# Interleaved stationary operands and a moving operand read from last to first, in a float32r decoder block on one core

## The chip, the cores and the metric

The kernel runs on one core of a Trainium2 chip. The metric is device time in microseconds (us) of one execution; times shown are the median of several runs. The profile shows one execution with every instruction on each engine: PE is the matmul engine (TensorE), PEld its loads of the stationary operand, ACT is ScalarE, DVE is VectorE, POOL is GpSimd, SPq the queue from which most DMAs are issued.

## The reference

One decoder layer over 256 tokens with a model width of 2048, all in float32. In order:

```python
x = x + 0.5 * swiglu(rmsnorm(x, ffn1_norm[i]), ffn1_w_gate[i], ffn1_w_up[i], ffn1_w_down[i])
h = rmsnorm(x, mix_norm[i])
proj = h @ w_in[i]
dq, dk, dv, hq, hf, hi, hg, gate_a, gate_b = jnp.split(proj, split_points, axis=-1)
...
y_a = diff_attention(dq, dk, dv, q_norm[i], k_norm[i], lam, rel_bias, diff_subln[i], lambda_init)
y_b = hgrn2(hq, hf, hi, hg, lower_bounds[i], hgrn_norm[i])
merged = jax.nn.sigmoid(gate_a) * (y_a @ w_branch_a[i]) + jax.nn.sigmoid(gate_b) * (y_b @ w_branch_b[i])
x = x + merged @ w_out[i]
x = x + 0.5 * swiglu(rmsnorm(x, ffn2_norm[i]), ffn2_w_gate[i], ffn2_w_up[i], ffn2_w_down[i])
ple = rmsnorm(p[i] @ w_ple_proj[i], ple_post_norm[i])
x = x + jax.nn.sigmoid(rmsnorm(x, ple_gate_norm[i]) @ w_ple_gate[i]) * ple
```

The feed-forward width is 5632; attention and the gated recurrence (hgrn2) have 8 heads of width 128 each.

## The kernel before

**Tiling.** Every large product has 256 tokens, in two token tiles of 128 (`NT`, index `tt`), and streams its weights from memory in blocks of 256 x 512 numbers (512 KB): two k tiles (`k2`) of 128 rows, 512 output columns (`NB`). The activations are the stationary operand, 128 features x 128 tokens for a k tile and a token tile; the weights are the moving operand, 128 x 512, read from column 0 to 511; the result, 128 tokens x 512 columns, gathers in one PSUM bank (`acc`).

**Precision.** Each number is split into a high float32r part and the rest. ScalarE writes the high part (`wh` for weights, line 114; names in H such as `AH`, `hH`, `yaH`, `ybH`, `mH`, `pH` for activations), VectorE the rest (`wl`, line 115; names in L). A product takes three matmuls: high by high (line 148), high by low (149), low by high (150).

**Order.** The schedule is written by hand. A table, `plan`, lists all 804 blocks in the order of their use: gate and up of the first feed-forward part (`gu1`, 176 blocks), `down1` (88), the columns of `w_in` for the mixing part (18 chunks of 8 blocks), `w_a` (16), then `w_in` and `w_b` by turns (32 and 16), `w_out` (32), `gu2` (176), `down2` (88), and `w_pg` and `w_pp` for the embedding (32 and 4). `prep` brings a block in and splits it `AHEAD` = 3 blocks before `group` multiplies it with 12 matmuls. Between blocks, small tasks (evacuations, transposes, attention heads, recurrence levels) are advanced by one step each.

**The last product.** Column chunk 3 of `w_pg` is done by `last_product`: there the second token tile goes in two halves of 256 columns into banks of the pool `ms`, so its matmuls read 128 x 256 moving columns.

**Layout of the stationary operands.** `new_act` and others allocate a tile [128, k tiles, 256 tokens]: the 128 tokens of a token tile lie side by side, 4 bytes apart, 512 bytes for a token tile. They are written by `split` (lines 182 to 187) from a PSUM bank of transposed activations (`tp`), or at the start from the tile `junk` that holds the transposed input. `two_k_tiles` calls `split` for two k tiles at once (512 elements for a partition) where there is no gain, for one (256 elements) where there is. `branch_input` (lines 358 to 364) calls it with a gain for two k tiles at once.

Of the kernel before, what the change touches and what calls it, by code (L numbers as in the profile page):

```python
# [11 lines left out]
F32R = mybir.dt.float32r  # L12
# [8 lines left out]
P = 128  # L21
SEQ = 256
NT = SEQ // P
D = 2048
KD = D // P
DFF = 5632
NH = 8
# [21 lines left out]
def block_kernel(ctx: ExitStack, tc: tile.TileContext, a: dict, out: bass.AP):  # L49
    nc = tc.nc  # L50
# [11 lines left out]
    def T(pool, shape, tag, dt=F32, **kw):  # L62
        uid[0] += 1
        return pool.tile(shape, dt, tag=tag, name=f"{tag}_{uid[0]}", **kw)

    def tcol(tt):
        return slice(tt * P, (tt + 1) * P)

    def ccol(c):
        return slice(c * NB, (c + 1) * NB)  # L70


    plan = []

# [63 lines left out]

    WHOLE = slice(0, NB)

    def group(n, act, last, dsts):
        AH, AL = act
        wh, wl = ready[n]
        for k2 in range(2):
            kt = 2 * plan[n][2] + k2
            for dst, tt, cols in dsts:
                hi, lo = AH[:, kt, tcol(tt)], AL[:, kt, tcol(tt)]
                nc.tensor.matmul(dst, hi, wh[:, k2, cols], start=(kt == 0), stop=False)  # L148
                nc.tensor.matmul(dst, hi, wl[:, k2, cols], start=False, stop=False)  # L149
                nc.tensor.matmul(dst, lo, wh[:, k2, cols], start=False, stop=(kt == last))  # L150

    def stream(w, c, groups, act, dsts, held=0):
        for g in range(groups - held):
# [25 lines left out]


    def split(H, L, src, gain=None):
        if gain is None:
            nc.scalar.copy(H, src)  # L183
            nc.vector.tensor_tensor(L, src, H.bitcast(F32), op=ALU.subtract)  # L184
        else:
            nc.scalar.activation(H, src, AF.Copy, scale=gain)  # L186
            nc.vector.scalar_tensor_tensor(L, src, gain, H.bitcast(F32), op0=ALU.mult, op1=ALU.subtract)
# [32 lines left out]
        return tp  # L220

    def new_act():
        return T(base, [P, KD, SEQ], "AH", F32R), T(base, [P, KD, SEQ], "AL", F32R)

    def new_ss4():
        return T(base, [P, NT, 4], "ss4", bufs=2)
# [19 lines left out]

    def ffn(gu, down, act, gain_next):
        with tc.tile_pool(name=gu, bufs=1) as fp:
            hH = T(fp, [P, DFF // P, SEQ], "hH", F32R)
            hL = T(fp, [P, DFF // P, SEQ], "hL", F32R)  # L250

            def hidden(acc, c):
                if c == 0 and rs[0] is None:
                    early = T(fp, [P, NT, NB], "early")
                    for tt in range(NT):
                        nc.scalar.copy(early[:, tt, :], acc[tt])
                    acc = [early[:, tt, :] for tt in range(NT)]
                while rs[0] is None:
                    yield
                h = []  # L260
                for tt in range(NT):
                    s = T(fp, [P, HALF], "s", bufs=2)
                    nc.scalar.activation(s, acc[tt][:, :HALF], AF.Silu, scale=rs[0][:, tt : tt + 1])  # L263
                    h.append(T(fp, [P, HALF], "h", bufs=4))
                    nc.vector.scalar_tensor_tensor(  # L265
                        h[tt], acc[tt][:, HALF:], rs[0][:, tt : tt + 1], s, op0=ALU.mult, op1=ALU.mult
                    )
                yield
                two_k_tiles(lambda tt, kt: h[tt][:, (kt - 2 * c) * P : (kt - 2 * c + 1) * P], hH, hL, 2 * c)

            for c in range(DFF // HALF):
                acc = product(gu, c, KG, act)
                spawn(hidden(acc, c))
            nact = new_act()
            ss4 = new_ss4()
            for c in range(D // NB):
                acc = product(down, c, FG, (hH, hL))
                spawn(residual(acc, c, 0.5, ss4, nact, gain_next, set_rs if c == 3 else None))
        return nact
# [51 lines left out]
    mp = mid.enter_context(tc.tile_pool(name="mid", bufs=1))  # L331
    GA = T(mp, [P, NT, D], "GA")
    V = T(mp, [P, NT, NH * VD], "V")
    yaH = T(mp, [P, NH, SEQ], "yaH", F32R)
    yaL = T(mp, [P, NH, SEQ], "yaL", F32R)
    nc.vector.tensor_scalar(gsub, small[:, S_SUB : S_SUB + 1], 1.0 - LAMBDA_INIT, None, op0=ALU.mult)

    def mix(m):
# [2 lines left out]
    def rcol(tt):  # L341
        return rs[0][:, tt : tt + 1]
# [14 lines left out]
    def branch_input(y, H, L, gain):  # L357
        for k in range(0, NH, 2):
            tp = T(psT, [P, 2, SEQ], "tp")
            for i in range(2):  # L360
                for tt in range(NT):
                    nc.tensor.transpose(tp[:, i, tcol(tt)], y[:, tt, (k + i) * P : (k + i + 1) * P], ident)  # L362
            split(H[:, k : k + 2, :], L[:, k : k + 2, :], tp, gain)
            yield

    with tc.tile_pool(name="att", bufs=1) as ap:
# [337 lines left out]
        drain()  # L704

    with tc.tile_pool(name="mrg", bufs=1) as gp:
        ybH = T(gp, [P, NH, SEQ], "ybH", F32R)
        ybL = T(gp, [P, NH, SEQ], "ybL", F32R)
        mH = T(gp, [P, KD, SEQ], "mH", F32R)
        mL = T(gp, [P, KD, SEQ], "mL", F32R)  # L710
        gb = [T(gp, [P, NB], f"gb{tt}") for tt in range(NT)]

        def gate_b(acc):
            for tt in range(NT):
                nc.scalar.activation(gb[tt], acc[tt], AF.Sigmoid, scale=rcol(tt))
            yield

        def branch_b(acc, c):
            for tt in range(NT):
                nc.vector.tensor_tensor(gb[tt], gb[tt], acc[tt], op=ALU.mult)  # L720
                nc.vector.tensor_tensor(GA[:, tt, ccol(c)], GA[:, tt, ccol(c)], gb[tt], op=ALU.add)
            yield
            for k in (0, 2):
                two_k_tiles(lambda tt, kt: GA[:, tt, kt * P : (kt + 1) * P], mH, mL, 4 * c + k)
                if k == 0:
                    yield

        spawn(branch_input(SG, ybH, ybL, small[:, S_HG : S_HG + 1]))
        for c in range(4):
            spawn(gate_b(mix(f"b{c}")))  # L730
            acc = product("w_b", c, HG, (ybH, ybL))
            spawn(branch_b(acc, c))
        act = new_act()
        ss4 = new_ss4()
        for c in range(4):
            acc = product("w_out", c, KG, (mH, mL))
            spawn(residual(acc, c, 1.0, ss4, act, gains[:, G_FFN2], set_rs if c == 3 else None))
# [6 lines left out]
    with tc.tile_pool(name="ple", bufs=1) as pp:  # L744
        pT = T(pp, [P, 2, SEQ], "pT")
        nc.gpsimd.dma_start(pT, a["pT"])
        gpost = T(pp, [P, D], "gpost")
        nc.gpsimd.dma_start(gpost, a["ple_post"].partition_broadcast(P))
        pact = (T(pp, [P, 2, SEQ], "pH", F32R), T(pp, [P, 2, SEQ], "pL", F32R))
        pg = T(pp, [P, NT, D], "pg")  # L750
        pss = new_ss4()
        pr = [None]

        def split_p():
            yield
            split(*pact, pT)

        def embed(acc, c):
            for tt in range(NT):
                square_sum(pss[:, tt, c : c + 1], acc[tt])  # L760
                nc.vector.tensor_tensor(pg[:, tt, ccol(c)], acc[tt], gpost[:, ccol(c)], op=ALU.mult)
            if c == 3:
                r = row_rms(pss)
                yield
                yield
                for tt in range(NT):
                    nc.vector.tensor_scalar(pg[:, tt, :], pg[:, tt, :], r[:, tt : tt + 1], None, op0=ALU.mult)
                pr[0] = r
            yield

        def finish_chunk(dsts, c, queue):
            o = []
            for acc, tt, cols in dsts:
                o.append(T(pp, [P, NB], "o", bufs=4)[:, : cols.stop - cols.start])
                nc.scalar.activation(o[-1], acc, AF.Sigmoid, scale=rcol(tt))
            while pr[0] is None:
                yield
            for t, (_, tt, cols) in zip(o, dsts):
                xs = slice(c * NB + cols.start, c * NB + cols.stop)
                nc.vector.tensor_tensor(t, t, pg[:, tt, xs], op=ALU.mult)  # L780
                nc.vector.tensor_tensor(t, t, x[:, tt, xs], op=ALU.add)
                queue.dma_start(out[tcol(tt), xs], t)

        def gate_chunk(c):
            acc = product("w_pg", c, KG, act)
            spawn(finish_chunk([(acc[tt], tt, WHOLE) for tt in range(NT)], c, nc.gpsimd))

        spawn(split_p())
        for c in (0, 1):
            gate_chunk(c)  # L790
            for c2 in (2 * c, 2 * c + 1):
                spawn(embed(product("w_pp", c2, 1, pact), c2))
        gate_chunk(2)
        for d in last_product("w_pg", 3, KG, act):
            spawn(finish_chunk([d], 3, nc.sync))
        drain()
# [99 lines left out]
```

## Time and profile before

| | us |
|---|---|
| median of 3 runs | 2307.64 (2307.3 to 2307.93) |
| profiled execution, its own time | 2307.12 |
| span of that execution, first to last instruction | 2304.2 |
| PE busy (matmuls) | 2296.5 |
| PEld busy (loads of the stationary operand) | 1903.1 |
| VectorE busy | 1270.9 |
| ScalarE busy | 1041.0 |

The granted clock of PE was 1.000 over the whole span. DMA brought in 432.55 MB, 188 GB/s in the mean. A matmul's busy time holds its passage through a pipeline, so that two matmuls overlap in the record; what a matmul costs in a dense stretch is read from the distance between the starts of two neighbours, not from its duration. The same holds for a load of the stationary operand.

### The profile page before, as it was taken

What the parts mean: (1) busy time and instruction counts of PE and PEld (TensorE: products, weight loads), DVE (VectorE), ACT (ScalarE), POOL (GpSimd) and SP (SyncE); (2) the same over time, 40 slices, a digit from 0 to 9 for tenths busy, and PEclk for the clock granted to TensorE, in tenths of its full rate; (3) what the DMA queues carried; (4) which work ended last, traced back from release to release, by engine and by line L of the source; (5) the groups of instructions that cost most, each with busy time, mean ns of one, the idle gap of its engine ahead of it and who ended that gap; (6) DMA issues with size and microseconds to landing.
All of it is one profiled execution on the core that took longest, in us unless ns stands there. A gap on an engine that the chain in (4) does not pass through costs nothing.

```text
span 2304.2 us, 27206 instructions
## 1 busy us (share of the span) xinstructions
PE 2296.5 (100%) x10564; PEld 1903.1 (83%) x10564; DVE 1270.9 (55%) x1381; ACT 1041.0 (45%) x1270; POOL 39.4 (2%) x38
## 2 busy tenths in 40 slices
PE   9999999999999999999999999999999999999999
PEld 7888888888888888888888888888888888888887
DVE  5555555544444576667765555545555555444456
ACT  6444444444444455553334444544444444344454
POOL 0000000000000100000000000000000000000000
PEclk9999999999999999999999999999999999999999
DMA  8666666666666655554555666666666656666664
GB/s 295 192 190 192 187 189 191 185 192 190 190 186 196 204 159 168 186 173 154 160 159 181 186 189 184 184 192 191 191 186 190 192 186 191 192 190 191 192 211 150
DMA packets 120464, 432.55 MB, mean 188 GB/s; under 512 B 13773, under 2 KB 14181, under 8 KB 120208
## 3 DMA queue, kind: packets, MB, share of 16 engines
q1 hardware_dynamic: 118800, 426.33, 59.7%
q0 software_dynamic: 1248, 4.43, 0.5%
q8 instruction: 82, 1.34, 0.2%
q14 instruction: 46, 0.38, 0.0%
q10 hardware_dynamic: 288, 0.07, 0.0%
HBM read 428.67 MB, written 2.11 MB: 187 GB/s over the span
## 4 chain that ended last, share of the span: by engine, by line
PE 98%; DMA 1%; DVE 0%; ACT 0%; SPq 0%; issue 0%; ACTq 0%
PE acc L148 31%; PE acc L150 31%; PE acc L149 31%; PE tp L209 1%; PE ms L616 1%; DMA raw<-in_gu 1%; PE tp L219 0%; PE ms L440 0%; PE ms L149 0%; PE ms L150 0%; PE ms L148 0%; PE ms L589 0%; PE tp L362 0%; ACT wh L114 0%; PE tp L477 0%
## 5 line engine op out<-in xcount | busy, mean ns | idle before, releaser
L115 DVE TENSOR_TENSOR wl<-raw,wh 128x1024 fp32r<-128x1024 f32 (+1 forms) x805 | 984.1, 1224 | 877.8 <-ACT wh L114 875.6
L114 ACT CAST wh<-raw 128x1024 fp32r<-128x1024 f32 (+1 forms) x805 | 843.8, 1049 | 932.3 <-PE acc L150 904.6
L148 PE MATMUL acc<-wh,AH 128*128 128x512 f32 x2224 | 878.8, 395 | 0.7 <-ACT wh L114 0.5
L150 PE MATMUL acc<-wh,AL 128*128 128x512 f32 x2224 | 868.4, 390 | 0.0
L149 PE MATMUL acc<-wl,AH 128*128 128x512 f32 x2224 | 866.9, 390 | 1.2 <-DVE wl L115 1.0
L150 PEld LDWEIGHTS acc<-wh,AL 128*128 128x128 f32 x2224 | 417.6, 188 | 88.5
L149 PEld LDWEIGHTS acc<-wl,AH 128*128 128x128 f32 x2224 | 418.4, 188 | 85.9 <-DVE wl L115 2.8
L148 PEld LDWEIGHTS acc<-wh,AH 128*128 128x128 f32 x2224 | 418.0, 188 | 85.1 <-ACT wh L114 1.6
L148 PE MATMUL acc<-wh,hH 128*128 128x512 f32 x704 | 275.6, 392 | 0.0
L150 PE MATMUL acc<-wh,hL 128*128 128x512 f32 x704 | 274.5, 390 | 0.0
L149 PE MATMUL acc<-wl,hH 128*128 128x512 f32 x704 | 274.2, 390 | 0.0
L149 PEld LDWEIGHTS acc<-wl,hH 128*128 128x128 f32 x704 | 132.3, 188 | 27.3
L150 PEld LDWEIGHTS acc<-wh,hL 128*128 128x128 f32 x704 | 132.2, 188 | 27.4
L148 PEld LDWEIGHTS acc<-wh,hH 128*128 128x128 f32 x704 | 132.2, 188 | 27.0
L263 ACT ACTIVATE s<-acc,rowr 128x256 f32<-128x256 f32 x86 | 40.6, 475 | 48.9 <-PE acc L150 48.9
L183 ACT CAST hH<-tp 128x512 fp32r<-128x512 f32 x44 | 25.8, 587 | 73.9 <-PE tp L209 73.9
L184 DVE TENSOR_TENSOR hL<-tp,hH 128x512 fp32r<-128x512 f32 x44 | 30.4, 692 | 45.9 <-ACT hH L183 45.8
L265 DVE SCALAR_TENSOR_TENSOR h<-acc,rowr,s 128x256 f32<-128x256 f32 x86 | 41.5, 484 | 19.4 <-ACT s L263 19.4
L148 PE MATMUL acc<-wh,mH 128*128 128x512 f32 x128 | 50.7, 396 | 0.0
L150 PE MATMUL acc<-wh,mL 128*128 128x512 f32 x128 | 50.0, 391 | 0.0
L149 PE MATMUL acc<-wl,mH 128*128 128x512 f32 x128 | 49.9, 390 | 0.0
L186 ACT ACTIVATE AH<-tp,gains 128x256 fp32r<-128x256 f32 x48 | 22.8, 475 | 30.5 <-PE tp L209 16.5
(191 smaller groups left out, 1018.2 us busy)
## 6 DMA issues: line engine op xcount, KB each, us to landing
raw<-in_gu SPq DMA_DIRECT2D x351, 512.0 KB, 3.6
raw<-in_down SPq DMA_DIRECT2D x176, 512.0 KB, 3.9
raw<-in_w_in SPq DMA_DIRECT2D x176, 512.0 KB, 3.6
raw<-in_w_out SPq DMA_DIRECT2D x32, 512.0 KB, 3.9
raw<-in_w_pg SPq DMA_DIRECT2D x32, 512.0 KB, 4.1
raw<-in_w_a SPq DMA_DIRECT2D x16, 512.0 KB, 3.5
raw<-in_w_b SPq DMA_DIRECT2D x16, 512.0 KB, 3.6
junk<-in_xT SPq DMA_DIRECT2D x8, 256.0 KB, 3.5
```

Of the source, the lines that this page charges most:

```text
L114: nc.scalar.copy(wh[:, ks, :], raw[:, ks, :])
L115: nc.vector.tensor_tensor(wl[:, ks, :], raw[:, ks, :], wh[:, ks, :].bitcast(F32), op=ALU.subtract)
L148: nc.tensor.matmul(dst, hi, wh[:, k2, cols], start=(kt == 0), stop=False)
L149: nc.tensor.matmul(dst, hi, wl[:, k2, cols], start=False, stop=False)
L150: nc.tensor.matmul(dst, lo, wh[:, k2, cols], start=False, stop=(kt == last))
L183: nc.scalar.copy(H, src)
L184: nc.vector.tensor_tensor(L, src, H.bitcast(F32), op=ALU.subtract)
L186: nc.scalar.activation(H, src, AF.Copy, scale=gain)
L209: nc.tensor.transpose(tp[:, i, tcol(tt)], src_of(tt, kt + i), ident)
L263: nc.scalar.activation(s, acc[tt][:, :HALF], AF.Silu, scale=rs[0][:, tt : tt + 1])
L265: nc.vector.scalar_tensor_tensor(h[tt], acc[tt][:, HALF:], rs[0][:, tt : tt + 1], s, op0=ALU.mult, op1=ALU.mult)
L616: nc.tensor.matmul(lp[:, i, tt, :], km[:, i, tt, :], q4[:, i, tt, :], start=True, stop=True)
```

## The change

Three things are edited.

**Layout.** A helper, `pairs`, allocates each stationary tile as [128, k tiles, 128, 2] and hands out a view with the axes swapped: the two token tiles lie interleaved, so that neighbouring tokens of one token tile are 8 bytes apart, with a token of the other tile between them. All stationary tiles use it: `AH`, `AL`, `hH`, `hL`, `yaH`, `yaL`, `ybH`, `ybL`, `mH`, `mL`, `pH`, `pL`. Their size stays the same.

**Writers.** `split` reshapes its source so that the order of the tokens agrees; what it writes now goes in steps of 8 bytes. `branch_input` calls it for each k tile by itself, so that 8 writes of 512 elements become 16 of 256 on ScalarE, and likewise on VectorE.

**Readers.** In `group`, for the blocks of `w_in`, `w_a`, `w_b`, `w_out` and `down2`, the moving operand is read from its last column to its first, and the result is written to the bank from last to first, so each number lands where it did. The blocks of `gu1`, `down1`, `gu2`, `w_pg` and `w_pp` go onward as before.

```diff
+    def pairs(pool, k, tag):
+        return T(pool, [P, k, P, NT], tag, F32R).rearrange("p k n t -> p k t n")
...
+    ONWARD, BACK = slice(None, None, 1), slice(None, None, -1)
+
     def group(n, act, last, dsts):
...
             for dst, tt, cols in dsts:
-                hi, lo = AH[:, kt, tcol(tt)], AL[:, kt, tcol(tt)]
-                nc.tensor.matmul(dst, hi, wh[:, k2, cols], start=(kt == 0), stop=False)
-                nc.tensor.matmul(dst, hi, wl[:, k2, cols], start=False, stop=False)
-                nc.tensor.matmul(dst, lo, wh[:, k2, cols], start=False, stop=(kt == last))
+                hi, lo = AH[:, kt, tt, :], AL[:, kt, tt, :]
+                way = BACK if plan[n][0] in ("w_in", "w_a", "w_b", "w_out", "down2") else ONWARD
+                whw, wlw = wh[:, k2, cols][:, way], wl[:, k2, cols][:, way]
+                nc.tensor.matmul(dst[:, way], hi, whw, start=(kt == 0), stop=False)
+                nc.tensor.matmul(dst[:, way], hi, wlw, start=False, stop=False)
+                nc.tensor.matmul(dst[:, way], lo, whw, start=False, stop=(kt == last))
...
     def split(H, L, src, gain=None):
+        if len(src.shape) == 3:
+            src = src.rearrange("p k (t n) -> p k t n", t=NT)
+        else:
+            src = src.rearrange("p (t n) -> p t n", t=NT)
...
     def new_act():
-        return T(base, [P, KD, SEQ], "AH", F32R), T(base, [P, KD, SEQ], "AL", F32R)
+        return pairs(base, KD, "AH"), pairs(base, KD, "AL")
...
-            hH = T(fp, [P, DFF // P, SEQ], "hH", F32R)
-            hL = T(fp, [P, DFF // P, SEQ], "hL", F32R)
+            hH = pairs(fp, DFF // P, "hH")
+            hL = pairs(fp, DFF // P, "hL")
...
-            split(H[:, k : k + 2, :], L[:, k : k + 2, :], tp, gain)
+            for i in range(2):
+                split(H[:, k + i, :], L[:, k + i, :], tp[:, i, :], gain)
```

The tiles `yaH`, `yaL`, `ybH`, `ybL`, `mH`, `mL`, `pH` and `pL` are allocated with `pairs` in the same way.

No instruction changes its place among the others, and no DMA changes. The only rows that differ in kind are those of the writers. ScalarE where the recurrence's result (`SG`) is transposed into `ybH`, between casts of weight blocks; before:

```order
L114 CAST wh_9375<-raw_9374 128x1024
L186 ACTIVATE ybH_9398<-tp_9404,small_93 128x512
L114 CAST wh_9414<-raw_9413 128x1024
L186 ACTIVATE ybH_9398<-tp_9431,small_93 128x512
L114 CAST wh_9439<-raw_9438 128x1024
```

and ScalarE at the same place with the change (the `x2` at the end of a row says that the row stands for two instructions):

```order
L117 CAST wh_9383<-raw_9382 128x1024
L197 ACTIVATE ybH_9406<-tp_9412,small_93 128x2x128 x2
L117 CAST wh_9424<-raw_9423 128x1024
L197 ACTIVATE ybH_9406<-tp_9441,small_93 128x2x128 x2
L117 CAST wh_9451<-raw_9450 128x1024
```

Each writer stands where it stood; one of 512 elements has become two of 2 x 128.

More of the change, by code (lines that the diff above doesn't have):

```diff
@@ L333, in block_kernel @@
     V = T(mp, [P, NT, NH * VD], "V")
-    yaH = T(mp, [P, NH, SEQ], "yaH", F32R)
-    yaL = T(mp, [P, NH, SEQ], "yaL", F32R)
+    yaH = pairs(mp, NH, "yaH")
+    yaL = pairs(mp, NH, "yaL")
     nc.vector.tensor_scalar(gsub, small[:, S_SUB : S_SUB + 1], 1.0 - LAMBDA_INIT, None, op0=ALU.mult)
@@ L706, in block_kernel @@
     with tc.tile_pool(name="mrg", bufs=1) as gp:
[L707 to L710, printed above, removed]
+        ybH = pairs(gp, NH, "ybH")
+        ybL = pairs(gp, NH, "ybL")
+        mH = pairs(gp, KD, "mH")
+        mL = pairs(gp, KD, "mL")
         gb = [T(gp, [P, NB], f"gb{tt}") for tt in range(NT)]
@@ L748, in block_kernel @@
         nc.gpsimd.dma_start(gpost, a["ple_post"].partition_broadcast(P))
-        pact = (T(pp, [P, 2, SEQ], "pH", F32R), T(pp, [P, 2, SEQ], "pL", F32R))
+        pact = (pairs(pp, 2, "pH"), pairs(pp, 2, "pL"))
         pg = T(pp, [P, NT, D], "pg")
```

## The prediction

> **What bounds the kernel now.** I first read the page's shares and its chain of work that ended last.
>
> ```profile
> span 2304.2 us, 27206 instructions
> PE 2296.5 (100%) x10564; PEld 1903.1 (83%) x10564; DVE 1270.9 (55%) x1381; ACT 1041.0 (45%) x1270; POOL 39.4 (2%) x38
> PE 98%; DMA 1%; DVE 0%; ACT 0%; SPq 0%; issue 0%; ACTq 0%
> ```
>
> The matmul engine is the chain: 98% of the span is PE's own work, and no other engine is at more than 55%. So the time is the number of matmuls times the distance between their starts, and an edit matters if it changes that distance or makes PE wait. The groups by line and shape give the number: 9600 matmuls with 512 moving columns and 96 with 256. These rows are the largest of them:
>
> ```profile
> L148 PE MATMUL acc<-wh,AH 128*128 128x512 f32 x2224 | 878.8, 395 | 0.7 <-ACT wh L114 0.5
> L148 PE MATMUL acc<-wh,hH 128*128 128x512 f32 x704 | 275.6, 392 | 0.0
> L148 PE MATMUL ms<-wh,AH 128*128 128x256 f32 x32 | 9.0, 281 | 0.0
> L148 PEld LDWEIGHTS acc<-wh,AH 128*128 128x128 f32 x2224 | 418.0, 188 | 85.1 <-ACT wh L114 1.6 <-ACT AH L186 0.6
> ```
>
> In 2224 matmuls PE idled 0.7 us: weights and activations are always there in time.
>
> The distance comes from the chain in order of time, where each chunk of 96 matmuls begins with four transposes:
>
> ```profile
> 77.66 0.44 PE tp L209 x4
> 99.88 0.44 PE tp L209 x4
> ```
>
> (99.88 - 77.66 - 0.44) / 96 = 0.2269 us for a matmul of 512 columns. Its record lasts 390 ns, but a neighbour starts after 227. Is that distance set by the moving columns or by the load of the stationary operand? The timeline of the last product, where matmuls of 256 columns stand between those of 512, answers:
>
> ```profile
> 2284.68 0.28 PE L148 MATMUL ms<-wh,AH 128*128 128x256 f32 x1
> 2284.79 0.28 PE L149 MATMUL ms<-wl,AH 128*128 128x256 f32 x1
> 2284.80 0.19 PEld L150 LDWEIGHTS ms<-wh,AL 128*128 128x128 f32 x1
> 2284.91 0.28 PE L150 MATMUL ms<-wh,AL 128*128 128x256 f32 x1
> 2285.39 0.40 PE L148 MATMUL acc<-wh,AH 128*128 128x512 f32 x1
> ```
>
> Six matmuls of 256 columns start in 2285.39 - 2284.68 = 0.71 us, 0.118 each, each with its own load. A load is recorded with 0.19 us, yet the matmul that needs it starts 0.11 after the load does. So a contiguous load is ready in 0.118 us or less, and under a 512-column matmul at least 0.227 - 0.118 = 0.109 us is left over: the moving columns set the distance, the load is hidden.
>
> **The change part by part.**
>
> *The instructions.* PE, SP and POOL issue the same rows in the same order; nothing is removed, no queue is passed, no wait is added. What can change is how long an access with another step takes. There are four kinds.
>
> *Stationary loads in steps of 8 bytes: all 9696.* No load of the trace has a step, so I bound it. Below: nothing, since it is hidden already. Above: the nearest rows of a doubled access are VectorE's predicated copies of the recurrence, with element runs of 1 (step 8 bytes) and of 64 over the same number of elements:
>
> ```profile
> 1029.31 1.32 DVE L620 COPY_PREDICATED A<-masks,ms 128x512 f32<-128x512 int32 x1 [2.15 <-PE ms L616]
> 1091.09 0.74 DVE L620 COPY_PREDICATED A<-masks,ms 128x512 f32<-128x512 int32 x1 [0.52 <-PE ms L616]
> ```
>
> A doubled load would take 2 x 0.118 = 0.236 us: 0.009 over the distance, 9600 x 0.009 = 86 us, and the 96 short matmuls, which cover only 0.118, would add 96 x 0.118 = 11 us; 97 us in all. With the ratio of these two rows, 1.32 / 0.74 = 1.78, it is 0.210 us: hidden under 512 columns, and 96 x 0.092 = 9 us for the short ones. But a moving operand is itself proof of what PE reads: it passes over 2048 bytes of a partition in 0.227 us, 9.0 bytes a ns; an interleaved stationary tile lies over 1024 bytes, and at 0.118 us that is 8.7 bytes a ns. No higher rate of bytes passed over is asked than PE shows. I take 0.
>
> [...]
>
> *Reversed moving reads and reversed PSUM writes.* `w_in` 176 blocks, `w_a` 16, `w_b` 16, `w_out` 32, `down2` 88: 328 blocks x 12 = 3936 matmuls, 41% of all. Nothing in the trace runs backwards on PE. Below: a 512-column matmul costs 0.2269, two of 256 cost 0.236, so 0.0091 of each matmul is there whatever its columns; more than that can't go without a faster column. 3936 x 0.0091 = 36 us is the most that reversal could give, and with the 9600 all of it 87 us. Above: the nearest row of a 512-column matmul at half pace is the warm-up, whose loads go one for each matmul:
>
> ```profile
> 2.48 0.15 PEld L290 LDWEIGHTS <-warm 128*128 128x128 bf16 x1 [0.28 <-issue]
> 2.91 0.15 PEld L290 LDWEIGHTS <-warm 128*128 128x128 bf16 x1 [0.28 <-issue]
> ```
>
> 0.43 us a matmul, 0.20 more than 0.227: 3936 x 0.20 = 787 us. These ends are far apart. [...]
>
> [...]
>
> *Writers in steps of 8 bytes.* VectorE has done this already: line 609 works on every second element at the first level, in runs of 64 at the last, both in 0.69:
>
> ```profile
> 1024.37 0.69 DVE L609 TENSOR_TENSOR S<-S,f 128x512 f32<-128x512 f32 x1
> 1088.02 0.68 DVE L609 TENSOR_TENSOR S<-S,f 128x512 f32<-128x512 f32 x1
> ```
>
> So VectorE's writers cost what they cost. ScalarE shows no such row; its writers are mainly these:
>
> ```profile
> L183 ACT CAST hH<-tp 128x512 fp32r<-128x512 f32 x44 | 25.8, 587 | 73.9 <-PE tp L209 73.9
> L186 ACT ACTIVATE AH<-tp,gains 128x256 fp32r<-128x256 f32 x48 | 22.8, 475 | 30.5 <-PE tp L209 16.5
> ```
>
> Doubled at worst, they would add 25.8 + 22.8 = 49 us (and the smaller groups a few more) to an engine that idles 55% of the span and whose results are used late: `ybH` below. 0 on the path. At the start, before PE is fed, the chain passes twice through VectorE's rest of the transposed input:
>
> ```profile
> 10.71 0.33 DVE AL L187
> 11.11 0.49 DVE AL L187
> 11.62 0.33 SPq L301
> 11.99 4.60 DMA raw<-in_gu
> ```
>
> SP waits for it before it reuses the input's buffer, and the weights behind it land later. The two passages are 0.33 + 0.49 and 0.07 + 0.49 us, 1.4 us; doubled, they cost 1.4 us. By line 609 I take 0.
>
> *Eight writers cut in two.* In `branch_input` an activation of 512 elements (0.689) becomes two of 256 (0.475 each by the row of `AH` above): +0.26 us on ScalarE, eight times, and about as much on VectorE. What hides it: the writers of `ybH` run from 1241.6 to 1251.2, the first matmul that reads it starts 1264.6, behind the first chunk of gate columns; `yaH` is written over 200 us before its use.
>
> ```profile
> L148 PE MATMUL acc<-wh,ybH x64: 388/389/390, 1264.6 to 1375.6; 128*128 128x512 f32 x64
> L186 ACT ACTIVATE ybH<-tp,small x4: 689/689/690, 1241.6 to 1251.2; 128x512 fp32r<-128x512 f32 x4
> ...
> L148 PE MATMUL acc<-wh,yaH x64: 388/390/475, 1192.7 to 1240.3; 128*128 128x512 f32 x64
> ...
> L186 ACT ACTIVATE yaH<-tp,small x4: 688/689/691, 957.0 to 966.7; 128x512 fp32r<-128x512 f32 x4
> ```
>
> Without the cover of 13 us it would be 8 x 0.26 = 2 us. Here, 0.
>
> **Sum.** 0 + 0 + 0 + 0 on 2307.12, the profiled execution's own time (its span of 2304.2 and 2.9 around it). The median of the runs shown is 0.5 higher; I forecast 2307.5. About 0.2%, 4.6 us, is what a measurement of this kernel can tell from no change.
>
> **The rivals.**
>
> *A load that leaves its cover* (slower). If an interleaved load takes about twice as long, the 512-column matmuls are held from the point where it exceeds 0.227 us; below it only the 96 short ones pay. For it: the predicated copy does double at that step. Against it: line 609 doesn't, and the byte rate above. 2317 at the ratio of 1.78 (9 us), 2405 when doubled (97 us). Chance 0.10.
>
> *Reversal at half pace* (slower). [...] Chance 0.17.
>
> *A toll for each reversed matmul* (slower). If only the start of a reversed access costs, by as much as the fixed part of 0.0091 again, it is +36 us: 2343. Chance 0.08, for anything up to a tenth of the distance.
>
> *The fixed part goes* (faster). If those 0.0091 us came from load and moving read meeting in the same place, the new layout might part them: 2271 if only the reversed ones gain, 2220 if all do. For it: the fixed part exists, and no row tells its source. Against it: nothing ties it to where operands lie, and loads already have 0.109 us to spare. Chance 0.07.
>
> **How the numbers follow.** Forecast 0.58, the load 0.10, half pace 0.17, toll 0.08, faster 0.07. The range takes in the forecast, the load up to its double, the toll, and half of the faster case (reversal alone, 36 us): 0.58 + 0.10 + 0.08 + 0.04 = 0.80, from 2270 to 2405; half pace is left out. Faster 0.07, within 0.2% 0.58, slower 0.35.
>
> **What would show it.** In the changed profile the distance between starts, from a chunk of `gu1` (interleaved, onward) and one of `w_in` or `down2` (interleaved, reversed). Both at 0.227 with PE at 98% of the chain: every step right. `gu1` and `gu2` longer: the load, to be seen also in records above 188 ns and in the short matmuls above 0.118. Only `w_in`, `w_a`, `w_b`, `w_out` and `down2` longer while `down1` stays: reversal, and `down1` against `down2` gives its price, since they differ in nothing else. PE waiting for ScalarE or VectorE: the writers were not hidden. The forecast is wrong if any of these moves by 1% of 0.227.

## The result, and the profile after

| | before | after |
|---|---|---|
| median of 3 runs, us | 2307.64 (2307.3 to 2307.93) | 2379.94 (2379.81 to 2380.6) |
| ratio, with its 95% interval | 1 | 1.0314 (1.0291 to 1.0338) |
| profiled span, us | 2304.2 | 2377.6 |

The change makes the kernel 72.3 us slower. The forecast was no change, with 0.35 for slower, so its direction was wrong. That the time lies in the range is luck: the upper end of the range was set by a load that takes twice as long, and the experiments show no such load in the changed kernel. None of the rivals gives this time by its own mechanism either.

The page of the changed kernel begins as that of before did (the granted clock of PE is again 1.000):

```profile
span 2377.6 us, 27220 instructions
PE 2369.9 (100%) x10564; PEld 1976.3 (83%) x10564; DVE 1274.8 (54%) x1389; ACT 1045.4 (44%) x1278; POOL 39.5 (2%) x38
PE 99%; DMA 0%; DVE 0%; SPq 0%; ACT 0%; issue 0%
```

PE's own work is still nearly the whole chain, and it grew by 2369.9 - 2296.5 = 73.4 us, exactly what the span grew by. So nothing new is waited for; the matmuls themselves stand further apart. The groups by line and shape of the changed kernel say the same (the count, then busy us and mean ns, then idle time ahead of them):

```profile
L155 PE MATMUL acc<-wh,AH 128*128 128x512 f32 x2224 | 893.0, 402 | 0.9 <-ACT wh L117 0.9
L155 PE MATMUL acc<-wh,hH 128*128 128x512 f32 x704 | 281.8, 400 | 0.0
L155 PEld LDWEIGHTS acc<-wh,AH 128*128 128x128 f32 x2224 | 434.2, 195 | 86.1 <-ACT wh L117 2.2 <-ACT AH L197 0.6
L194 ACT CAST hH<-tp 128x512 fp32r<-128x512 f32 x44 | 27.1, 617 | 77.6 <-PE tp L220 77.6
```

PE's idle time in the largest group went from 0.7 to 0.9 us only. A load's record went from 188 to 195 ns, a writer of `hH` from 587 to 617.

The distance between starts comes from the chain of the changed kernel. Three neighbouring chunk boundaries of `gu1` (96 matmuls a chunk), two of `down1` and two of `down2` (264 matmuls and two sets of transposes a chunk):

```profile
102.37 0.44 PE tp L220 x4
125.21 0.44 PE tp L220 x4
148.27 0.44 PE tp L220 x4
...
639.72 0.44 PE tp L220 x4
...
702.77 0.44 PE tp L220 x4
...
2146.35 0.44 PE tp L220 x4
...
2209.71 0.44 PE tp L220 x4
```

`gu1`: (22.84 - 0.44) / 96 = 0.2333 us in one chunk, (23.06 - 0.44) / 96 = 0.2356 in the next. `down1`: (63.05 - 0.88) / 264 = 0.2355. `down2`: (63.36 - 0.88) / 264 = 0.2367. Before, it was 0.2269.

That is the point to see: `gu1` and `down1` are interleaved but not reversed, and have most of the loss already.

The table gives every stage: the mean distance between the starts of two neighbouring 512-column matmuls with nothing between them, in ns, from the starts in the trace (distances over 260 ns, at waits and right behind a break, are left out). Its last two columns belong to the first two experiments.

| stage | matmuls | before | after | growth x count, us | layout alone | reversal alone |
|---|---|---|---|---|---|---|
| `gu1` | 2112 | 227.0 | 233.8 | 14.4 | 233.8 | 227.1 |
| `down1` | 1056 | 226.9 | 234.9 | 8.4 | 234.9 | 226.9 |
| `w_in` | 2112 | 228.0 | 235.7 | 16.4 | 233.5 | 233.4 |
| `w_a` | 192 | 227.2 | 233.4 | 1.2 | 233.3 | 233.3 |
| `w_b` | 192 | 226.7 | 236.7 | 1.9 | 233.3 | 233.3 |
| `w_out` | 384 | 227.6 | 236.6 | 3.5 | 233.5 | 233.4 |
| `gu2` | 2112 | 227.0 | 233.9 | 14.6 | 233.9 | 227.0 |
| `down2` | 1056 | 226.9 | 236.7 | 10.3 | 234.9 | 233.3 |
| `w_pg` | 336 | 227.5 | 235.4 | 2.7 | 235.5 | 227.4 |

The growths add up to 73.4 us, and the 48 matmuls of `w_pp`, which are not in the table, add 0.4 (from 226.7 to 235.6 ns). The span grew by 73.4: the distance explains the whole loss.

### The profile page after: what moved, and what is told of

Its sections match the earlier page's. It is cut to its first block, busy times and chain, and to the rows that moved or that the text cites. A ratio compares the mean times of both kernels' runs of the same rounds, so it can differ in the third digit from the quotient of the medians.

```text
span 2377.6 us, 27220 instructions
## 1 busy us (share of the span) xinstructions
PE 2369.9 (100%) x10564; PEld 1976.3 (83%) x10564; DVE 1274.8 (54%) x1389; ACT 1045.4 (44%) x1278; POOL 39.5 (2%) x38
## 4 chain that ended last, share of the span: by engine, by line
PE 99%; DMA 0%; DVE 0%; SPq 0%; ACT 0%; issue 0%
PE acc L155 32%; PE acc L156 32%; PE acc L157 32%; PE tp L220 1%; PE ms L628 1%; PE tp L230 0%; DMA raw<-in_gu 0%; PE ms L452 0%; PE ms L157 0%; PE ms L156 0%; PE ms L155 0%; PE ms L601 0%; PE tp L373 0%; PE tp L490 0%; PE ms L653 0%; PE tp L489 0%
## 5 line engine op out<-in xcount | busy, mean ns | idle before, releaser
L155 PE MATMUL acc<-wh,AH 128*128 128x512 f32 x2224 | 893.0, 402 | 0.9 <-ACT wh L117 0.9
L156 PE MATMUL acc<-wl,AH 128*128 128x512 f32 x2224 | 880.8, 396 | 1.0 <-DVE wl L118 1.0
L157 PE MATMUL acc<-wh,AL 128*128 128x512 f32 x2224 | 881.4, 396 | 0.0
L157 PEld LDWEIGHTS acc<-wh,AL 128*128 128x128 f32 x2224 | 433.4, 195 | 89.2
L155 PEld LDWEIGHTS acc<-wh,AH 128*128 128x128 f32 x2224 | 434.2, 195 | 86.1 <-ACT wh L117 2.2
L156 PEld LDWEIGHTS acc<-wl,AH 128*128 128x128 f32 x2224 | 433.7, 195 | 83.8 <-DVE wl L118 1.6
L155 PE MATMUL acc<-wh,hH 128*128 128x512 f32 x704 | 281.8, 400 | 0.0
L157 PE MATMUL acc<-wh,hL 128*128 128x512 f32 x704 | 280.3, 398 | 0.0
L157 PEld LDWEIGHTS acc<-wh,hL 128*128 128x128 f32 x704 | 138.0, 196 | 28.7
L155 PEld LDWEIGHTS acc<-wh,hH 128*128 128x128 f32 x704 | 138.4, 197 | 26.8
```

The source lines that it names most:

```text
L155: nc.tensor.matmul(dst[:, way], hi, whw, start=(kt == 0), stop=False)
L156: nc.tensor.matmul(dst[:, way], hi, wlw, start=False, stop=False)
L157: nc.tensor.matmul(dst[:, way], lo, whw, start=False, stop=(kt == last))
```

## The experiments

Each kernel was run in turns with the kernel before on the same chip. The diffs are against the changed kernel; "onward" means that no moving operand is reversed.

### The two halves of the change

**Layout alone.** All blocks go onward.

```diff
-                way = BACK if plan[n][0] in ("w_in", "w_a", "w_b", "w_out", "down2") else ONWARD
+                way = ONWARD
```

> The interleaved layout with every moving operand read onward. Theory L (the longer loads of the stationary operand carry nearly the whole loss): about 2374 us, with the matmul distance of w_in, w_out and down2 falling from 235.6-236.7 ns to about that of down1, 234-235 ns, and gu1 staying at 233.9 ns. Theory R (reversal carries a good part of it): 2345 us or less. Theory W (the writers in steps of 8 bytes make PE wait): still near 2380 us, with PE idle in the waits.

Measured: 2372.61 us against 2307.98, ratio 1.028 (1.0266 to 1.0295): +64.6. So theory L came, as to the share of the loss. Its chain, two boundaries of `down1` and two of `down2`:

```profile
640.68 0.44 PE tp L220 x4
...
703.74 0.44 PE tp L220 x4
...
2139.56 0.44 PE tp L220 x4
...
2202.61 0.44 PE tp L220 x4
```

(63.06 - 0.88) / 264 = 0.2355 us in `down1`, as in the changed kernel, and (63.05 - 0.88) / 264 = 0.2355 in `down2`: without reversal the two stages are alike.

**Reversal alone.** The stationary tiles are contiguous again.

```diff
     def pairs(pool, k, tag):
-        return T(pool, [P, k, P, NT], tag, F32R).rearrange("p k n t -> p k t n")
+        return T(pool, [P, k, NT, P], tag, F32R)
```

> The old contiguous layout (the cut writers of branch_input kept), moving operands reversed as in the change. Theory L: 2307 us, within 0.2% of before, with 226.7 ns in down2 as in down1. Theory R with a price of its own for a reversed matmul, 1.1 to 1.8 ns as between down1 and down2 of the change: 3936 x 1.1 to 1.8 = 2312 to 2315 us. Theory R in full: 2340 us or more.

Measured: 2330.22 us, ratio 1.0096 (1.0082 to 1.011): +22.2, between the expected price of its own (2312 to 2315 us) and theory R in full. The chain of this kernel, two boundaries of `down1` and two of `down2`:

```profile
622.69 0.44 PE tp L220 x4
...
683.53 0.44 PE tp L220 x4
...
2101.62 0.44 PE tp L220 x4
...
2164.10 0.44 PE tp L220 x4
```

(60.84 - 0.88) / 264 = 0.2271 us in `down1`, which is as before, and (62.48 - 0.88) / 264 = 0.2333 in `down2`. These two stages differ in the reversal only, so its price is about 6.2 ns a matmul by these boundaries, 6.4 by the table.

Together the two would give 64.6 + 22.2 = 86.8 us; the change costs 72.3. Where both apply, the distance is not 2 x 6.7 ns longer but at 235.7 to 236.7 ns, and in `w_a` at 233.4, no longer than with either alone. The two prices do not add: the second finds most of the distance raised already. Why that is so no run shows.

### Reading or writing backwards

With the contiguous layout, either the moving operand alone is reversed, or the result alone.

```diff
...
-                nc.tensor.matmul(dst[:, way], hi, whw, start=(kt == 0), stop=False)
-                nc.tensor.matmul(dst[:, way], hi, wlw, start=False, stop=False)
-                nc.tensor.matmul(dst[:, way], lo, whw, start=False, stop=(kt == last))
+                nc.tensor.matmul(dst, hi, whw, start=(kt == 0), stop=False)
+                nc.tensor.matmul(dst, hi, wlw, start=False, stop=False)
+                nc.tensor.matmul(dst, lo, whw, start=False, stop=(kt == last))
```

> Contiguous layout; in the five reversed stages only the moving operand is read from last to first, the result is written onward (so the columns of those products lie mirrored, the output is not the reference's). If the reading side carries reversal's 6.7 ns: 233.3 ns in those stages and 2330 us. If the writing side carries it: 226.7 ns and 2308 us. If it is only that both run down: 2308 us here and in the next run.

```diff
...
-                whw, wlw = wh[:, k2, cols][:, way], wl[:, k2, cols][:, way]
+                whw, wlw = wh[:, k2, cols], wl[:, k2, cols]
```

> Contiguous layout; in the five reversed stages the moving operand is read onward and only the result is written from last to first (columns of those products mirrored). If the writing side carries it: 233.3 ns and 2330 us. If the reading side: 226.7 ns and 2308 us.

Measured against 2308.16 us: reading backwards 2329.91, ratio 1.0097 (1.0079 to 1.0115), +21.8; writing backwards 2307.57, ratio 0.9999 (0.9989 to 1.0008). The chains show two boundaries of `down2` each, first reading, then writing:

```profile
2101.15 0.44 PE tp L220 x4
...
2163.63 0.44 PE tp L220 x4
```

```profile
2081.45 0.44 PE tp L220 x4
...
2142.29 0.44 PE tp L220 x4
```

(62.48 - 0.88) / 264 = 0.2333 and (60.84 - 0.88) / 264 = 0.2271: the price of reversal is all in the read from SBUF. Here the direction of writing in PSUM is free.

### Is it the length of the load?

**Low tiles alone.** Only the tiles of the low parts are interleaved: one of three matmuls takes its load from them.

```diff
     def pairs(pool, k, tag):
+        if tag.endswith("H"):
+            return T(pool, [P, k, NT, P], tag, F32R)
...
-                way = BACK if plan[n][0] in ("w_in", "w_a", "w_b", "w_out", "down2") else ONWARD
+                way = ONWARD
```

> Only the L tiles interleaved, the H tiles contiguous, all onward: one load in three has a step. If each stepped load costs by itself: a third of the layout's 67 us, 2330 us, and the distance is longer only from the matmul of line 156 to that of line 157, whose load it is. If the price hangs on the stream as a whole (a phase that all loads share): near 2307 or near 2374 us, and equal on all three lines.

Measured: 2343.23 us, ratio 1.0153 (1.0139 to 1.0167): +35.3, over half of the layout's 64.6. That is neither a third of it nor near one of the ends, as the expectations had it. All three kinds of matmul stand further apart: 230.9, 230.0 and 232.5 ns behind high by high, high by low and low by high, though only the loads from low tiles have changed (194 ns in their record; the others stay at 188):

```profile
L159 PEld LDWEIGHTS acc<-wh,AL 128*128 128x128 f32 x2224 | 431.6, 194 | 96.8
L158 PEld LDWEIGHTS acc<-wl,AH 128*128 128x128 f32 x2224 | 418.5, 188 | 96.4 <-DVE wl L120 3.1
```

So a load changes the distance of matmuls that don't use it, which speaks for a state of the whole stream and against a toll on each such load.

**A step of 16 bytes.** Two k tiles are woven with the two token tiles, so that neighbours are 16 bytes apart; onward. (The class `Woven`, which picks a k tile out of such a pair, and the line `way = ONWARD` are left out of the diff.)

```diff
...
     def pairs(pool, k, tag):
-        return T(pool, [P, k, P, NT], tag, F32R).rearrange("p k n t -> p k t n")
+        return Woven(T(pool, [P, k // min(k, 2), P, min(k, 2), NT], tag, F32R))
...
```

> Two k tiles woven together with the two token tiles: stationary steps of 16 bytes, all onward, same memory. If the price follows the bytes that a load passes over (512 before, 1024 in the change, now 2048): 3 times the added 6.9 ns, so 9600 x 20.6 = 198 us, 2505 us. If any step other than 4 bytes costs the same: 2374 us. [...]

Measured: 2413.41 us, ratio 1.0457 (1.0443 to 1.0472): +105.4. That is more than if any step cost the same (2374 us) and less than if the price went by the bytes passed over (2505 us). Its group of loads, and the 256-column matmuls of the last product in its timeline:

```profile
L168 PEld LDWEIGHTS acc<-wl,AH 128*128 128x128 f32 x2224 | 692.5, 311 | 2.3 <-DVE wl L130 2.2
```

```profile
2373.27 0.40 PE L169 MATMUL ms<-wh,AL 128*128 128x256 f32 x1
2373.50 0.40 PE L167 MATMUL ms<-wh,AH 128*128 128x256 f32 x1
2373.74 0.40 PE L168 MATMUL ms<-wl,AH 128*128 128x256 f32 x1
```

Set beside them the same place of the changed kernel:

```profile
2358.13 0.28 PE L157 MATMUL ms<-wh,AL 128*128 128x256 f32 x1
2358.25 0.28 PE L155 MATMUL ms<-wh,AH 128*128 128x256 f32 x1
2358.37 0.28 PE L156 MATMUL ms<-wl,AH 128*128 128x256 f32 x1
2358.49 0.28 PE L157 MATMUL ms<-wh,AL 128*128 128x256 f32 x1
2358.61 0.40 PE L155 MATMUL acc<-wh,AH 128*128 128x512 f32 x1
```

At a step of 8 bytes a 256-column matmul takes 0.120 us with its load, as good as before (mean 0.1201 against 0.1188). So an interleaved load is ready in 0.120 us, half of what a 512-column matmul offers it: it does not leave its cover. At 16 bytes a short matmul takes 0.235: there the load takes twice as long and sets the distance of the short ones by itself. This is also longer than the 0.227 of the long ones before, so at this step the load has left its cover, and the long matmuls stand at its pace (235.0 ns in `gu1`, 235.8 in `down1`). Over all stages they are some 8.2 ns longer than before, which makes 8.2 ns x 9600 = 79 us; the short matmuls add 96 x 0.114 = 11 us, and the first matmul behind each set of transposes starts after 433 to 443 ns, where the changed kernel has 327. So the rival of the load that leaves its cover exists, but at 16 bytes. At 8 bytes nearly the same distance, 233.3 to 235.6 ns, comes about with a load that needs half the time, and needs another cause.

**A step of 32 bytes.** Four k tiles are woven in the same way (`min(k, 4)`).

> Four k tiles woven together: stationary steps of 32 bytes, all onward. [...]

Measured: 2500.47 us, ratio 1.0836 (1.0818 to 1.0854): +192.5, with 244.3 to 245.5 ns by stage. Its loads:

```profile
L169 PEld LDWEIGHTS acc<-wh,AL 128*128 128x128 f32 x2224 | 732.5, 329 | 0.0
```

The short matmuls stand at 0.240 us. From 16 to 32 bytes the bytes passed over double, but the load slows by little (0.235 to 0.240 us, 311 to 329 ns in its record), and the long matmuls follow it (235.0 ns in `gu1` and 235.8 in `down1` at 16 bytes).

**One number for the whole load.** The stationary operand repeats its first number (step 0); the layout is contiguous, everything onward.

```diff
...
-                hi, lo = AH[:, kt, tt, :], AL[:, kt, tt, :]
-                way = BACK if plan[n][0] in ("w_in", "w_a", "w_b", "w_out", "down2") else ONWARD
+                hi, lo = (t[:, kt, tt, 0:1].to_broadcast([P, P]) for t in (AH, AL))
+                way = ONWARD
```

> Everything onward, contiguous tiles, but each load of the stationary operand reads its first number 128 times (step 0), so the activations are left out of the products. Theory B (the load's and the moving operand's reads meet in the memory, and the 13.3 ns that each matmul takes beyond 512 columns come from that): those 13.3 ns shrink, 215 to 220 ns, 2200 to 2245 us. Theory P (what counts is whether the load's pattern is plain, steps of 4 bytes): any other step gives 233.3 ns or more, 2373 us. If neither, 226.7 ns and 2308 us.

Measured: 2335.61 us, ratio 1.0121 (1.0105 to 1.0137): +27.5. The loads keep their 188 ns, the short matmuls are even closer (0.113 us), and still the long ones are at 229.4 to 231.7 ns. A load that passes over four bytes costs more than one that passes over 512: the bytes passed over are not the measure. None of the three expected times came: the distance neither shrinks, as theory B had it, nor reaches 233.3 ns, as theory P had it.

### Is it where load and moving read lie?

**The same steps at other addresses.** Contiguous, onward, but the token tiles of `hH` and `hL` are 528 bytes apart instead of 512. No access has another step than before.

```diff
     def pairs(pool, k, tag):
-        return T(pool, [P, k, P, NT], tag, F32R).rearrange("p k n t -> p k t n")
+        if tag in ("hH", "hL"):
+            return T(pool, [P, k, NT, P + 4], tag, F32R)[:, :, :, 0:P]
+        return T(pool, [P, k, NT, P], tag, F32R)
...
```

> Everything onward, contiguous stationary tiles in steps of 4 bytes, but in hH and hL each token tile starts 528 instead of 512 bytes after the one before, so addresses differ. Theory P: 226.7 ns in down1 and down2, 2308 us. Theory B, with addresses that decide: another distance in down1 and down2, 233.3 ns if it is as with the steps, 2112 x 6.7 = 14 us, 2322 us.

Measured: 2317.25 us, ratio 1.0042 (1.0026 to 1.0058): +9.1. `down1` and `down2` are at 231.6 ns, all other stages at what they had before, to a tenth of a ns. Two boundaries of its `down2`, (62.06 - 0.88) / 264 = 0.2317 us:

```profile
2089.32 0.44 PE tp L222 x4
...
2151.38 0.44 PE tp L222 x4
```

So theory P, by which only the step counts, fails. Within these stages the distance repeats every 4 blocks, that is 16 token tiles of 16 bytes each, which suggests a period of 256 bytes. The weight blocks also go through 4 buffers in turn (`bufs=4`); in the kernel before, where the loads' addresses do not shift, that rotation leaves the distance at 226.7 ns, but no run parts the two.

**Chosen shifts.** Contiguous and onward, but parts of `hH` and `hL` begin 0, 16, 32 and 64 bytes later in `down1`, and 48, 96, 128 and 192 in `down2` (counted in 4-byte numbers in the code).

```diff
...
+            b = first * SEQ + self.offsets[(first > 11) + (first > 21) + (first > 33)]
+            v = self.t[:, b : b + count * SEQ].rearrange("p (k t n) -> p k t n", t=NT, n=P)
...
+            offs = (0, 4, 8, 16) if gu == "gu1" else (12, 24, 32, 48)
+            hH = Shifted(T(fp, [P, DFF // P * SEQ + 64], "hH", F32R), offs)
...
```

> Everything onward, contiguous tiles in steps of 4 bytes; hH and hL are shifted by a constant that changes every 10 to 12 k tiles: 0, 16, 32, 64 bytes in down1, 48, 96, 128, 192 bytes in down2. Theory B1 (where load and moving operand stand to each other in the memory sets the distance): stretches with different steady distances, some perhaps below 226.7 ns. Theory B2 (the stream locks itself into the cheapest phase whenever all loads go alike, whatever the constant; only loads that differ from one to the next break it, as in padded): 226.7 ns in every stretch behind a short transition, 2308 to 2310 us.

Measured: 2316.31 us, ratio 1.0037 (1.0023 to 1.0052). The timeline of `down1` gives the distance for each shift. First two matmuls that stand 48 apart in the part shifted by 16 bytes, then two in the part shifted by 32:

```profile
576.80 0.39 PE L168 MATMUL acc<-wh,hH 128*128 128x512 f32 x1
...
587.68 0.39 PE L168 MATMUL acc<-wh,hH 128*128 128x512 f32 x1
...
593.20 0.40 PE L168 MATMUL acc<-wh,hH 128*128 128x512 f32 x1
...
604.40 0.40 PE L168 MATMUL acc<-wh,hH 128*128 128x512 f32 x1
```

10.88 / 48 = 0.2267 us and 11.20 / 48 = 0.2333. The load reads as many bytes in the same order, 16 bytes further on, and the matmul takes 6.7 ns longer. So theory B2 fails, as all loads of a part go alike. The load itself is not recorded as longer: over all parts its mean is that of the kernel before.

```profile
L168 PEld LDWEIGHTS acc<-wh,hH 128*128 128x128 f32 x704 | 132.5, 188 | 30.0
```

**Shifts under the change's two accesses.** In two kernels `down1` is interleaved and onward, `down2` contiguous and reversed, the rest as before; the parts are shifted by 16, 32, 64 and 96 bytes in the first (near), by 128, 160, 192 and 224 in the second (far).

```diff
...
+            offs, order = (4, 8, 16, 24), "n t" if gu == "gu1" else "t n"
+            hH = Shifted(T(fp, [P, DFF // P * SEQ + 64], "hH", F32R), offs, order)
...
-                way = BACK if plan[n][0] in ("w_in", "w_a", "w_b", "w_out", "down2") else ONWARD
+                way = BACK if plan[n][0] == "down2" else ONWARD
```

> All other tiles contiguous and onward. down1: interleaved hH and hL (steps of 8 bytes) read onward; down2: contiguous hH and hL with the moving operand reversed. Both shifted by 16, 32, 64, 96 bytes for 10 to 12 k tiles each. Theory B1 (the two readers' standing to each other in memory sets the distance): different steady distances, with some stretches of either stage well under 233 ns, so that the change's loss is one of address. Theory P2 (a stepped load, or a descending read, costs its 6.7 ns at any address): 233 ns or more in every stretch.

> The same with shifts of 128, 160, 192, 224 bytes. B1 and P2 as in the run before; by the period of 256 bytes that padded showed, these two runs hold what any shift can give in steps of 32 bytes. If some stretch lies under 226.7 ns, a layout exists that beats the kernel before.

Measured: 2319.47 us, ratio 1.0049 (1.0034 to 1.0064), and 2320.55, ratio 1.0055 (1.0038 to 1.0072). In the timeline of the near one, two matmuls 48 apart at a shift of 64 bytes, in `down1` and then in `down2`:

```profile
593.96 0.39 PE L168 MATMUL acc<-wh,hH 128*128 128x512 f32 x1
...
605.00 0.39 PE L168 MATMUL acc<-wh,hH 128*128 128x512 f32 x1
...
2059.18 0.40 PE L168 MATMUL acc<-wh,hH 128*128 128x512 f32 x1
...
2070.38 0.40 PE L168 MATMUL acc<-wh,hH 128*128 128x512 f32 x1
```

11.04 / 48 = 0.2300 us and 11.20 / 48 = 0.2333. So B1 came for the interleaved loads, P2 for the reversed reads. The distances in steady stretches, in ns, for all shifts:

| shift, bytes | contiguous, onward | interleaved, onward | contiguous, reversed |
|---|---|---|---|
| 0 | 226.7 | 233.3 to 235.6 | 233.3 |
| 16 | 226.7 | 233.3 | 233.3 |
| 32 | 233.3 | 231.9 to 233.3 | 233.3 |
| 48 | 233.3 | not run | not run |
| 64 | 233.3 | 230.0 | 233.3 |
| 96 | 234.2 | 230.0 (one chunk 233.3) | 233.3 |
| 128 | 232.0 to 232.8 | 231 to 231.7 | 233.3 |
| 160, 224 | not run | 233.3 | 233.3 |
| 192 | 228.9 | 233.3 | 233.3 |

By its address alone a contiguous load moves between 226.7 and some 234, an interleaved one between 230.0 and 235.6. A reversed read over contiguous loads stands at 233.3 wherever the load lies, also where an onward one had that already. No place and no layout that was run goes below the 226.7 of the kernel before, so no version here beats it.

## Why the forecast was wrong, point by point

**The bound was read rightly.** The time is the number of matmuls times the distance of their starts; the growth of that distance accounts for all of the 73.4 us, and no new wait is found.

**Stationary loads: the step that failed.** The prediction said of a contiguous load that "the moving columns set the distance, the load is hidden", and took 0 for the interleaved one. Both halves of its reading hold: the interleaved load is hidden (0.120 us or less, by the short matmuls), and PE can read at that rate. What does not follow is that a hidden load leaves the distance alone. The same load 16 bytes further on costs 6.7 ns, a load of one number costs 3 to 5 ns, and a changed load under one matmul lengthens the distance behind the others. The term was 0; it measured 64.6 us, within the bound of 97, but by another mechanism than the one that set the bound, a doubled load. That it fell inside is luck.

The byte rate did not exclude anything: it compared rates of the load and of the moving read as if each had SBUF to itself. The runs show that the distance also depends on where the load lies. Only the load was shifted, never the moving operand, so that it is the standing of the two to each other that counts is argued, not shown.

By the short matmuls the pace of the load is 0.120 us at a step of 8 bytes, 0.235 at 16 and 0.240 at 32. That a load of 0.120 us adds nothing to the matmuls above it was the prediction's estimate. The moving read is not independent of the load here: in the column of contiguous, onward loads above only the load's address differs, and the matmuls stand 226.7 to 234.2 ns apart.

**Reversal.** Taken as 0, with ends of -36 and +787 us. No run shows that 0: it measured +22.2 alone and 72.3 - 64.6, some 8 us, on top of the layout. The price is in the read (+21.8 us with the reading alone reversed): from 226.7 to 233.3 ns in steady stretches, 3% for each of 3936 matmuls. The sign that the prediction named for its price, `down1` against `down2`, shows 1.8 ns in the changed kernel, on top of the layout; alone it is 6.4. The rival of a toll (36 us) priced it nearest, as 9.1 ns a matmul, but gave the start of a reversed access as its cause; no run parts a toll at the start from one along the columns. Half pace is excluded: a reversed matmul takes 6.7 ns more, not 0.20 us. The other half of the term, reversed writing, was rightly 0: 2307.57 against 2308.16 us.

**The rival of the fixed part** had this for its condition: "if those 0.0091 us came from load and moving read meeting in the same place". That an address alone moves the distance, while the load's record stays at 188 ns, shows that a hidden load does affect the matmuls; that the two reads meet in one place is argued. But the layout could only lose by it: the kernel before already stands at the lowest value that any shift gave. Besides, the distance is 226.7 in steady stretches and a 256-column matmul most often 120 (44 of the 85 distances between short ones in the kernel before), so 256 columns take 106.7 ns and 13.3 ns are left over by this estimate, not 9.1. What the change adds is not a fixed part for each matmul either: a long one grows by 6.7 or more, a short one by 1.3 in the mean.

**Writers and the cut.** Hidden, as forecast. A writer of `hH` takes 30 ns longer, one of `AH` 24 (499 against 475). For the cut, the tile `ybH`:

```profile
L155 PE MATMUL acc<-wh,ybH x64: 399/400/400, 1302.3 to 1417.7; 128*128 128x512 f32 x64
...
L197 ACT ACTIVATE ybH<-tp,small x8: 501/508/513, 1278.5 to 1289.3; 128x256 fp32r<-128x256 f32 x8
```

Its last write starts at 1289.3, its first reader at 1302.3: the cover is 13 us still. At the start of the program the second chunk's first matmul comes 29.6 us after the first warm-up matmul, 28.6 before, and 30.4 in the kernel with the contiguous layout and reversal: no share of it can be put down to the writers.

**What stays open.** Whether the load and the moving read share a part of the memory, and which; and whether the period is 256 bytes. Why a stretch settles at 233.3 or at 235.6 ns: with the layout alone every fourth chunk of `gu1` is at the higher value, and with the reversal whole stages are, at 236.7. In `gu1` of the changed kernel each chunk at the higher value follows a break of 585 ns at the transposes, the others, but for one, a break of 586 to 589; no run set that phase by itself. That the two accesses meet in one place would fit the shifts; that is the author's guess, which no run shows.

## What to carry to other kernels

That a transfer into PE is shorter than the matmul above it doesn't show that it is free: here a load of 0.120 us under matmuls that start 0.227 us apart cost 64.6 us. Measure the distance between starts, stage by stage, for each layout and each address, since 3% of a matmul is 3% of such a kernel. Keep the stationary tiles and the moving operand contiguous and ascending (226.7 ns here, where interleaved loads gave 230.0 to 235.6 and reversed reads 233.3), and compare addresses too where tiles are padded or shifted (226.7 to 234.2). In this kernel the direction in which a result is written to PSUM could be chosen freely (2307.57 us against 2308.16).

## What the runs showed of the hardware that was not expected

- A contiguous load of 128 x 128 float32r changes the distance of 512-column matmuls from 226.7 to 233.3 ns when it is shifted by 32 bytes, and not when it is shifted by 16; its own record stays at 188 ns.
- In many stretches the distance takes sharp values. In the kernel before, the first one behind each set of transposes is over 310 ns, the next 3 to 10 lie between 224 and 236, and then it settles at 226.7.
- A load of one repeated number (step 0) is no gain: 188 ns in its record, and long matmuls 3 to 5 ns further apart.
- A load at a step of 16 bytes takes about twice as long as one at 8 (short matmuls at 0.235 against 0.120 us), while a step of 32 adds little more (0.240).
